# A planner that knows two more things about the chip: a port that VectorE and GpSimd share, and another pace of TensorE

## The chip, the core and the metric

The kernel runs on one core of a Trainium2 chip. A core has five engines with queues of their own: TensorE (PE: matmuls and transposes), VectorE (DVE), ScalarE (ACT), GpSimd (POOL) and SyncE (SP), which here issues most transfers. Each engine takes its instructions strictly in the order in which the program lists them, and an instruction whose operand isn't there yet holds up all behind it on that engine. The metric is the time of one execution in microseconds; the median of several runs counts.

## What is computed

One layer of a diffusion backbone over 1024 latent tokens of width 1024 and 256 context tokens, in float32:

```python
h, hc = modulate(rmsnorm(x)), modulate(rmsnorm(ctx))     # shifts, scales: silu(c) @ w_ada
q, k, v, z, xbc, dt, gates = split(h @ w_in)
o = diff_attention(rope(q), rope(k), v)                  # 8 heads, keys of context and latents
u = silu(dwconv3(xbc)); xs, B, C = split(u)              # SSD: 16 heads in 4 groups, chunks
y = scan_forward(xs, B, C, dt) + scan_backward(...) + d_skip * xs
y = group_rmsnorm(y * silu(z))
mix = (sig(ga) * (o @ w_attn) + sig(gs) * (y @ w_ssd)) @ w_out
x = x + gt1 * rmsnorm(mix)
f = shared_expert(h2) + top8_of_64_experts(h2)           # h2 = modulate(rmsnorm(x))
out = x + gt2 * rmsnorm(f)
```

## The kernel before

The program is one long stream in stages, which the profile shows one after the other: the modulation vectors and q, k, v (to about 400 us); the SSD **mixer** (400 to 1055); the branch projections and the attention (1055 to 1680); merge, output projection and routing (to about 1890); the mixture of experts (to 2745); the last norm and the output.

Products that need full float32 are made of three matmuls in F32R (a float32 operand is split into a high and a low part, `hi` and `lo`; `acc` gets `hh*hi`, `hl*hi` and `hh*lo`, 128x512 each). The split is an ACT copy for `hi` and a DVE or POOL subtraction for `lo`.

**What sets the order.** No order is written out by hand. Each piece of work is a generator (a *stream*) that yields what it needs next: tiles, free buffers of a ring, an engine. `Flow` keeps a model of time beside the program: `Flow.op` charges each operation to its engine's clock (`s.clk`) and notes when its result is ready. `Flow.run` resumes the stream that can go on first by that model (of those that can go on at once, the one with the lowest priority number), and whatever the stream issues is appended to the queues of its engines, under a manual schedule. So the numbers in `mm` (L137), `_dve`, `tt`, `ptt` and their like are never executed: they decide which instruction stands ahead of which. Two helpers also choose an engine by the clocks: `copy` (DVE or ACT) and `either`/`sub` (DVE or POOL).

**The mixer.** `server` (priority 3, so whenever nothing more urgent can go on) works off 41 jobs: columns of `w_in` for the convolution (`conv`), for `z` and for the gates (`g`). Its matmuls write `acc`: 3632 in F32R, besides those of `dt`. Once a group of heads has its convolved channels, `group` transposes them, and for each of four pairs (two heads by two halves of the sequence) spawns two `unit`s and one `products`. A unit works through

```python
F.stt(W[:, c], s.ge, dt[...], W[:, c], ...)     # x4, after 4 F.ts
F.ptt(G, Rv[0], ac[...], ALU.subtract)          # POOL, R loaded from acd
F.stt(G[:, c], Rv[1][:, c], ac[...], G[:, c], ...) # x4
F.ptt(W, W, CB[...], ALU.mult)                  # POOL
F.act(G, G, AF.Exp); F.tt(W, W, G, ALU.mult)
```

and its `decays` make `R` by an ACT exponential and a POOL product. `products` then issues a group of 24 float32 matmuls of 128 columns into `py` (48 records in the trace), which read both units' `W` and `R`; there are 16 such groups. Rings limit how far units run ahead: `G` and `W` have two buffers, `R` six. After a group, `evac` makes `yt`; after four, `norm` sums squares (`aux<-cst,G`), takes a reciprocal root on DVE (`rs_y`), spreads it with PE transposes (`aux<-cst,rs_y`) and stores `yn`. When all four head groups are through, `branches` opens: it loads `yn` and weights, splits them (`bxh`, `bxl`, `bwh`, `bwl`) and issues the `bacc` matmuls; `attention_ahead` loads `qk` through POOL's queue for the scores (`sps`).

Elsewhere `wacc` are DVE sums over rows of `w_ada` that PE adds up into `adab`, among the q, k, v matmuls; `tr<-cst,r` are transposes of rotated q and k; in the mixture of experts PE waits at times for a split of gathered tokens (`xl`) or of hidden values (`hl`).

Of the kernel before, what the change touches and what calls it, by code (L numbers as in the profile page):

```python
# [16 lines left out]
PSUM = bass.MemoryType.PSUM  # L17
# [56 lines left out]
def _n(ap):  # L74
    return ap.tensor.name


class Ring:


    def __init__(s, F, pool, shape, dt, name, n):
        s.F, s.pool, s.shape, s.dt, s.name, s.n = F, pool, shape, dt, name, n
        s.free, s.at = n, [0.0] * n
# [22 lines left out]
class Flow:  # L106
# [7 lines left out]
    def __init__(s, nc):  # L114
        s.nc = nc
        s.clk = {"PE": 0.0, "DVE": 0.0, "ACT": 0.0, "POOL": 0.0, "DMA": 0.0}
        s.ready, s.last, s.hold, s.streams, s.seq = {}, {}, {}, [], 0
        s.later, s.pend, s.now, s.fresh = [], {}, 0.0, {}

    def op(s, eng, dur, out, ins):  # L120
        if out is not None and _n(out) in s.pend:
            s.flush(src=_n(out))
        t = s.clk[eng]
        more = 55.0 if eng == "PE" else 0.0
        for a in ins:
            t = max(t, s.ready.get(_n(a), 0.0) + more)
        if out is not None:
            t = max(t, s.fresh.pop(_n(out), 0.0))
        e = t + dur
        s.clk[eng] = e  # L130
        for a in ins:
            s.last[_n(a)] = max(s.last.get(_n(a), 0.0), e)
        if out is not None:
            s.ready[_n(out)] = max(e + s.LAT[eng], s.ready.get(_n(out), 0.0) if eng == "DMA" else 0.0)
            s.last[_n(out)] = max(s.last.get(_n(out), 0.0), e)

    def mm(s, out, l, r, start, stop, d=None):  # L137
        n = r.free_size()
        if d is not None:
            pass  # L140
        elif l.dtype == F32:
            d = max(4 * n / 2.4, 213.0)
        elif l.dtype == F32R:
            d = n / 2.4 + 2 if n >= 256 else 107.0 if n >= 192 else 213.0
        else:
            d = max(n / 2.4, 27.0)
        s.nc.tensor.matmul(out, l, r, start=start, stop=stop)  # L147
        s.op("PE", d, out, (l, r))
# [14 lines left out]
        s.nc.scalar.copy(out, in_)  # L163
        s.op("ACT", (51 if in_.space == PSUM else 94) + 0.833 * out.free_size(), out, (in_,))

    def _dve(s, out, ins, rate=0.96, aps=0, base=65):
        s.op("DVE", base + 62 * aps + out.free_size() / rate, out, ins)

    def tt(s, out, a, b, op):
        s.nc.vector.tensor_tensor(out, a, b, op=op)  # L170
        s._dve(out, (a, b), base=69)

    def ptt(s, out, a, b, op):
        s.nc.gpsimd.tensor_tensor(out, a, b, op=op)
        s.op("POOL", 36 + 2.22 * out.free_size(), out, (a, b))

    def ts(s, out, a, s1, s2, op0, op1=None):
        if op1 is None:
            s.nc.vector.tensor_scalar(out, a, s1, s2, op0=op0)  # L179
        else:  # L180
            s.nc.vector.tensor_scalar(out, a, s1, s2, op0=op0, op1=op1)  # L181
        aps = [v for v in (s1, s2) if hasattr(v, "tensor")]
        s._dve(out, (a, *aps), 0.96 if a.space == PSUM else 1.92, len(aps))

    def stt(s, out, a, sc, b, op0, op1):
        s.nc.vector.scalar_tensor_tensor(out, a, sc, b, op0=op0, op1=op1)  # L186
        aps = (sc,) if hasattr(sc, "tensor") else ()
        s._dve(out, (a, b, *aps), aps=len(aps), base=69)

    def ts_reduce(s, out, a, s1, op0, op1, acc):  # L190

# [3 lines left out]

    def vcopy(s, out, a):
        s.nc.vector.tensor_copy(out, a)  # L197
        s._dve(out, (a,), 0.96 if a.space == PSUM else 1.92)

    def red(s, out, a, op):  # L200
        s.nc.vector.tensor_reduce(out, a, axis=AX.X, op=op)  # L201
# [2262 lines left out]
```

## Time and profile before

| what | value |
|---|---|
| three runs | 2828.54, 2836.93, 2843.67 us, median 2836.93 |
| the profiled execution | 2838.21 us, span of its trace 2836.1 us |
| mean granted clock of PE | 0.967 of full speed |
| PE busy | 2624.0 us, 93% of the span |
| DVE, ACT, POOL busy | 2000.2, 1339.9 and 882.9 us |
| DMA, 2250 to 2745 us | 96% of its engines' time, 304 GB/s |

The execution takes 2.1 us more than the span from its first to its last instruction. PE is busy nearly all the time, so the kernel's length is PE's work, plus the times that PE stands, plus what its matmuls lose at a lower clock. DVE, ACT and POOL stand often; that costs nothing unless PE waits for what they were late with.

### The profile page before, as it was taken

What the parts mean: (1) busy time and instruction counts of PE and PEld (TensorE: products, weight loads), DVE (VectorE), ACT (ScalarE), POOL (GpSimd) and SP (SyncE); (2) the same over time, 40 slices, a digit from 0 to 9 for tenths busy, and PEclk for the clock granted to TensorE, in tenths of its full rate; (3) what the DMA queues carried; (4) which work ended last, traced back from release to release, by engine and by line L of the source; (5) the groups of instructions that cost most, each with busy time, mean ns of one, the idle gap of its engine ahead of it and who ended that gap; (6) DMA issues with size and microseconds to landing.
All of it is one profiled execution on the core that took longest, in us unless ns stands there. A gap on an engine that the chain in (4) does not pass through costs nothing. (4 is left out here: it accounts for less than half of the span.)

```text
span 2836.1 us, 41280 instructions
## 1 busy us (share of the span) xinstructions
PE 2624.0 (93%) x14561; PEld 2109.4 (74%) x14561; DVE 2000.2 (71%) x4690; ACT 1339.9 (47%) x2105; POOL 882.9 (31%) x670
## 2 busy tenths in 40 slices
PE   7999979999999999999998899899999998999991
PEld 4777868878787776888887687678887776777660
DVE  6876123577776658888893657867788877787863
ACT  4211113344444445666673422335666656576641
POOL 0101010444454520000000000056656656666641
PEclk9999989999999999999999999999999999999995
DMA  7667242243424345224234853478899998999997
GB/s 278 211 205 201 84 127 84 75 130 93 134 82 138 101 133 183 88 84 145 92 101 152 266 164 109 184 247 250 278 310 302 316 302 266 308 305 312 327 306 212
DMA packets 275266, 544.89 MB, mean 192 GB/s; under 512 B 31546, under 2 KB 166819, under 8 KB 248050
## 3 DMA queue, kind: packets, MB, share of 16 engines
q1 hardware_dynamic: 238898, 435.31, 45.1%
q0 software_dynamic: 36160, 106.93, 14.8%
q8 instruction: 115, 1.88, 0.3%
q14 instruction: 93, 0.76, 0.1%
HBM read 432.99 MB, written 124.73 MB: 197 GB/s over the span
## 5 line engine op out<-in xcount | busy, mean ns | idle before, releaser
L170 DVE TENSOR_TENSOR gl<-raw,gh 128x1024 fp32r<-128x1024 f32 x240 | 288.3, 1218 | 40.4 <-ACT gh L163 40.2
L147 PE MATMUL acc<-hh,hi 128*128 128x512 f32 (+2 forms) x760 | 303.7, 400 | 1.4 <-DVE ux L186 1.4
L163 ACT CAST gh<-raw 128x1024 fp32r<-128x1024 f32 x240 | 247.6, 1051 | 101.2 <-PE gu L147 65.9
L147 PE MATMUL acc<-hl,hi 128*128 128x512 f32 (+2 forms) x760 | 287.8, 379 | 0.0
L147 PE MATMUL gu<-gh,xh 128*128 128x512 f32 (+3 forms) x672 | 280.7, 418 | 3.8 <-ACT xh L163 3.4
L147 PE MATMUL acc<-hh,lo 128*128 128x512 f32 (+1 forms) x736 | 279.3, 380 | 2.5 <-DVE lo L170 2.5
L147 PE MATMUL gu<-gl,xh 128*128 128x512 f32 (+3 forms) x672 | 266.7, 397 | 4.4 <-DVE gl L170 4.3
L147 PE MATMUL gu<-gh,xl 128*128 128x512 f32 (+3 forms) x672 | 266.9, 397 | 3.8 <-DVE xl L170 3.7
L261 POOL DMA_INDIRECT cr<-cumd,crow x98 | 124.8, 1273 | 440.7 <-DVE y L197 408.8
L192 DVE TENSOR_SCALAR_CACHE_REDUCE e<-sps 128x512 f32<-128x512 f32 (+1 forms) x384 | 214.2, 596 | 31.2 <-PE sps L147 31.0
L267 POOL DMA_INDIRECT yacc<-y,tk x98 | 180.4, 1841 | 86.3 <-issue 31.3
L147 PE MATMUL sps<-qk 128*128 128x512 f32 (+1 forms) x768 | 195.4, 385 | 8.2 <-DVE e L192 4.5
L155 ACT ACTIVATE e<-e,st 128x1280 f32<-128x1280 f32 x128 | 174.7, 1366 | 31.2 <-DVE st L201 31.0
L147 PE MATMUL acc<-hi,hh 128*128 128x512 f32 x448 | 183.3, 409 | 0.0
L261 POOL DMA_INDIRECT wc<-wtab,tk x98 | 137.9, 1407 | 141.3 <-DVE tk L181 93.9
L147 PE MATMUL acc<-hi,hl 128*128 128x512 f32 x448 | 177.3, 396 | 0.4 <-DVE hl L170 0.4
L147 PE MATMUL acc<-lo,hh 128*128 128x512 f32 x448 | 177.1, 395 | 0.0
L147 PEld LDWEIGHTS sps<-qk 128*128 128x128 f32 x768 | 140.0, 190 | 41.7 <-DVE e L192 10.8
L147 PEld LDWEIGHTS acc<-hh,hi 128*128 128x128 f32 (+1 forms) x760 | 143.5, 189 | 31.2 <-issue 3.7
L147 PE MATMUL pv<-wr,vv 128*128 128x256 f32 x640 | 164.2, 380 | 0.0
L147 PEld LDWEIGHTS acc<-hl,hi 128*128 128x128 f32 (+1 forms) x760 | 143.7, 189 | 25.3 <-issue 0.6
L147 PEld LDWEIGHTS acc<-hh,lo 128*128 128x128 f32 x736 | 139.6, 190 | 29.7 <-DVE lo L170 3.0
(323 smaller groups left out, 6253.7 us busy)
## 6 DMA issues: line engine op xcount, KB each, us to landing
raw<-in_w_e_gate_dram SPq DMA_DIRECT2D x64, 1024.0 KB, 10.6
raw<-in_w_e_up_dram SPq DMA_DIRECT2D x64, 1024.0 KB, 11.3
draw<-in_w_e_down_dram SPq DMA_DIRECT2D x64, 1024.0 KB, 10.0
qk<-qk POOLq DMA_DIRECT2D x16, 1664.0 KB, 8.4
raw<-in_w_in_dram SPq DMA_DIRECT2D x40, 512.0 KB, 4.6
wada<-in_w_ada_dram SPq DMA_DIRECT2D x32, 512.0 KB, 5.2
R<-acd SPq DMA_DIRECT2D x64, 256.0 KB, 5.4
qk<-sa SPq DMA_DIRECT2D x52, 256.0 KB, 4.3
```

Of the source, the lines that this page charges most:

```text
L147: s.nc.tensor.matmul(out, l, r, start=start, stop=stop)
L155: s.nc.scalar.activation(out, in_, fn, **kw)
L163: s.nc.scalar.copy(out, in_)
L170: s.nc.vector.tensor_tensor(out, a, b, op=op)
L192: s.nc.vector.tensor_scalar(out, a, s1, None, op0=op0, op1=op1, accum_out=acc)
L261: s.nc.gpsimd.indirect_dma_start(out=out, out_offset=None, in_=table, in_offset=bass.IndirectOffsetOnAxis(ap=idx, axis=0), **kw)
L267: s.nc.gpsimd.indirect_dma_start(out=table, out_offset=bass.IndirectOffsetOnAxis(ap=idx, axis=0), in_=in_, in_offset=None, compute_op=ALU. ...
```

## The change

`Flow` gets two more pieces of knowledge. `port` keeps the last eight intervals of each of DVE and POOL in which an operation holds the port that both use, and a new operation of the one starts, in the model, only after those of the other that it would overlap. Marked are POOL's `ptt` and, on DVE, `tt`, `stt`, `ts` and `vcopy` where no operand is in PSUM; not marked are reductions, reciprocals and indirect transfers. And an F32R matmul of n columns is charged (n+32)/2.4 ns in place of n/2.4+2: 226.7 in place of 215.3 for 512 columns. Nothing that is computed changes.

```diff
--- before.py
+++ after.py
@@ -115,9 +115,10 @@
         s.nc = nc
         s.clk = {"PE": 0.0, "DVE": 0.0, "ACT": 0.0, "POOL": 0.0, "DMA": 0.0}
         s.ready, s.last, s.hold, s.streams, s.seq = {}, {}, {}, [], 0
-        s.later, s.pend, s.now, s.fresh = [], {}, 0.0, {}
-
-    def op(s, eng, dur, out, ins):
+        s.later, s.pend, s.now, s.fresh, s.port = [], {}, 0.0, {}, {"DVE": [], "POOL": []}
+
+    def op(s, eng, dur, out, ins, port=False):
+
         if out is not None and _n(out) in s.pend:
             s.flush(src=_n(out))
         t = s.clk[eng]
@@ -126,6 +127,11 @@
             t = max(t, s.ready.get(_n(a), 0.0) + more)
         if out is not None:
             t = max(t, s.fresh.pop(_n(out), 0.0))
+        if port:
+            for a, b in sorted(s.port["POOL" if eng == "DVE" else "DVE"]):
+                if a < t + dur and t < b:
+                    t = b
+            s.port[eng] = s.port[eng][-7:] + [(t, t + dur)]
         e = t + dur
         s.clk[eng] = e
         for a in ins:
@@ -141,7 +147,7 @@
         elif l.dtype == F32:
             d = max(4 * n / 2.4, 213.0)
         elif l.dtype == F32R:
-            d = n / 2.4 + 2 if n >= 256 else 107.0 if n >= 192 else 213.0
+            d = (n + 32) / 2.4 if n >= 256 else 107.0 if n >= 192 else 213.0
         else:
             d = max(n / 2.4, 27.0)
         s.nc.tensor.matmul(out, l, r, start=start, stop=stop)
@@ -163,16 +169,16 @@
         s.nc.scalar.copy(out, in_)
         s.op("ACT", (51 if in_.space == PSUM else 94) + 0.833 * out.free_size(), out, (in_,))
 
-    def _dve(s, out, ins, rate=0.96, aps=0, base=65):
-        s.op("DVE", base + 62 * aps + out.free_size() / rate, out, ins)
+    def _dve(s, out, ins, rate=0.96, aps=0, base=65, port=False):
+        s.op("DVE", base + 62 * aps + out.free_size() / rate, out, ins, port)
 
     def tt(s, out, a, b, op):
         s.nc.vector.tensor_tensor(out, a, b, op=op)
-        s._dve(out, (a, b), base=69)
+        s._dve(out, (a, b), base=69, port=PSUM not in (a.space, b.space))
 
     def ptt(s, out, a, b, op):
         s.nc.gpsimd.tensor_tensor(out, a, b, op=op)
-        s.op("POOL", 36 + 2.22 * out.free_size(), out, (a, b))
+        s.op("POOL", 36 + 2.22 * out.free_size(), out, (a, b), True)
 
     def ts(s, out, a, s1, s2, op0, op1=None):
         if op1 is None:
@@ -180,12 +186,12 @@
         else:
             s.nc.vector.tensor_scalar(out, a, s1, s2, op0=op0, op1=op1)
         aps = [v for v in (s1, s2) if hasattr(v, "tensor")]
-        s._dve(out, (a, *aps), 0.96 if a.space == PSUM else 1.92, len(aps))
+        s._dve(out, (a, *aps), 0.96 if a.space == PSUM else 1.92, len(aps), port=a.space != PSUM)
 
     def stt(s, out, a, sc, b, op0, op1):
         s.nc.vector.scalar_tensor_tensor(out, a, sc, b, op0=op0, op1=op1)
         aps = (sc,) if hasattr(sc, "tensor") else ()
-        s._dve(out, (a, b, *aps), aps=len(aps), base=69)
+        s._dve(out, (a, b, *aps), aps=len(aps), base=69, port=PSUM not in (a.space, b.space))
 
     def ts_reduce(s, out, a, s1, op0, op1, acc):
 
@@ -195,7 +201,7 @@
 
     def vcopy(s, out, a):
         s.nc.vector.tensor_copy(out, a)
-        s._dve(out, (a,), 0.96 if a.space == PSUM else 1.92)
+        s._dve(out, (a,), 0.96 if a.space == PSUM else 1.92, port=a.space != PSUM)
 
     def red(s, out, a, op):
         s.nc.vector.tensor_reduce(out, a, axis=AX.X, op=op)
```

Instruction counts hardly change: PE's stay as they are, one `bwl` goes from DVE to POOL, three `Bn` copies from DVE to ACT and one `xn` copy the other way, and ACT loads its tables 71 times in place of 60. What changes is the order. Three places:

**PE among the q, k, v matmuls**, around the 12th `wacc` sum, which follows 372 F32R matmuls before (`acc` matmuls of one token tile, then the sum, then the next tile's):

```order
L147 MATMUL acc<-hi_732,hl_84 128x512
L147 MATMUL acc<-hi_732,hh_83 128x512
L147 MATMUL acc<-lo_733,hh_83 128x512
L147 MATMUL acc<-hi_732,hl_84 128x512
L147 MATMUL adab<-cst,wacc 128x1
L147 MATMUL acc<-hi_839,hh_83 128x512
L147 MATMUL acc<-lo_840,hh_83 128x512
L147 MATMUL acc<-hi_839,hl_84 128x512
```

and now, where it follows 384:

```order
L153 MATMUL acc<-lo_825,hh_83 128x512
L153 MATMUL acc<-hi_824,hl_84 128x512
L153 MATMUL acc<-hi_824,hh_83 128x512
L153 MATMUL acc<-lo_825,hh_83 128x512
L153 MATMUL acc<-hi_824,hl_84 128x512
L153 MATMUL acc<-hi_824,hh_83 128x512
L153 MATMUL acc<-lo_825,hh_83 128x512
L153 MATMUL acc<-hi_824,hl_84 128x512
L153 MATMUL adab<-cst,wacc 128x1
L153 MATMUL acc<-hi_732,hh_85 128x512
L153 MATMUL acc<-lo_733,hh_85 128x512
L153 MATMUL acc<-hi_732,hl_86 128x512
```

It stands 12 matmuls later. The fifth does too (240, now 252), and the 26th stands 36 later (612, now 648).

**PE at the mixer's end.** Before, the last product group follows 3449 conv and gate matmuls (`acc`), and 183 of them are left to stand behind it, around the norm's sums and transposes and around the first three branch matmuls; this is the piece with those:

```order
L147 MATMUL acc<-hh_85,hi 128x512
L147 MATMUL acc<-hl_86,hi 128x512
L147 MATMUL acc<-hh_85,lo 128x512
L147 MATMUL bacc<-bxh,bwh 128x512
L147 MATMUL bacc<-bxl,bwh 128x512
L147 MATMUL bacc<-bxh,bwl 128x512
L147 MATMUL acc<-hh_83,hi 128x512
L147 MATMUL acc<-hl_84,hi 128x512
L147 MATMUL acc<-hh_83,lo 128x512
```

Now all 3632 `acc` matmuls stand ahead of the third and the fourth group of the last four, which follow each other; after their 48 matmuls (the second group's last ones are shown) come the sums, the transposes and the branch matmuls with nothing between:

```order
L153 MATMUL py<-W,xn 64x128 x2
L153 MATMUL py<-R,hp_7664 64x128 x2
L153 MATMUL py<-R,hp_7665 64x128 x2
L153 MATMUL py<-W,xn 64x128 x2
L153 MATMUL py<-R,hp_7664 64x128 x2
L153 MATMUL py<-R,hp_7665 64x128 x2
L153 MATMUL aux<-cst,G 128x1 x8
L157 MATMUL aux<-cst,rs_y 128x128 x8
L153 MATMUL bacc<-bxh,bwh 128x512
L153 MATMUL bacc<-bxl,bwh 128x512
L153 MATMUL bacc<-bxh,bwl 128x512
```

Counted by the `acc` matmuls ahead of them, the four last groups stood at 3281, 3338, 3392 and 3449; now at 3497, 3578, 3632 and 3632. The twelve earlier ones are 48 to 191 later too (the first at 1985, was 1937), and the spacing inside a head group is 54 to 96, was 54 to 72.

**SP at the mixer's end.** Before, loads of weights (`raw`) and stores of gates (`gt`) stand around the stores of the normed result (`yn`):

```order
L211 DMA raw<-in_w_in_dram 128x8x128
L211 DMA gt_3154<-zg 128x512 x2
L211 DMA gt_3155<-zg 128x512
L211 DMA yn_3132<-yt 128x512
L211 DMA yn_3133<-yt 128x512
L211 DMA yn_3132<-yt 128x512
L211 DMA yn_3133<-yt 128x512
L211 DMA gt_3155<-zg 128x512
L211 DMA lv_8486<-in_lam_q_dram 128x64
L211 DMA lv_8487<-in_lam_k_dram 128x64
L211 DMA lv_8488<-in_lam_q_dram 128x64
L211 DMA lv_8489<-in_lam_k_dram 128x64
```

Now the last two loads of `R` (for the last unit) come right ahead of the stores of `yn`, and the gates are stored before:

```order
L217 DMA gt_3157<-zg 128x512
L217 DMA zg<-zs_3141 128x512
L217 DMA R<-acd_3124 128x512
L217 DMA R<-acd_3125 128x512
L217 DMA yn_3132<-yt 128x512
L217 DMA yn_3133<-yt 128x512
L217 DMA yn_3132<-yt 128x512
L217 DMA yn_3133<-yt 128x512
L217 DMA lv_8618<-in_lam_q_dram 128x64
L217 DMA lv_8619<-in_lam_k_dram 128x64
L217 DMA lv_8620<-in_lam_q_dram 128x64
L217 DMA lv_8621<-in_lam_k_dram 128x64
```

In the attention, the output projection and the mixture of experts the matmuls keep nearly the same distances from what they read: some sums of `xl` stand further ahead of their readers, some of `hl` a little nearer.

## Rows read from the trace of the kernel before

**Rows 1.** Page: span, and each engine's busy time.

```profile
span 2836.1 us, 41280 instructions
...
PE 2624.0 (93%) x14561; PEld 2109.4 (74%) x14561; DVE 2000.2 (71%) x4690; ACT 1339.9 (47%) x2105; POOL 882.9 (31%) x670
```

**Rows 2.** Windows: length, then PE, PEld, DVE, ACT, POOL busy, PEclk, DMA.

```profile
500.00:1055.00 555.00, 527.71 (x3039) 440.46 (x3037) 385.94 (x929) 243.83 (x350) 242.93 (x206) 0.98 0.35 108
...
2250.00:2745.00 495.00, 467.19 (x3134) 340.52 (x3134) 395.21 (x696) 312.20 (x486) 308.14 (x210) 0.98 0.96 304
```

**Rows 3.** Waits of PE, 500 to 1070: total us, times, longest.

```profile
PE py L147 <- DVE W L170: 14.0, 9, 2.9
PE py L147 <- POOL R L174: 8.0, 10, 3.3
PE acc L147 <- DVE lo L170: 2.5, 1, 2.5
```

**Rows 4.** Timeline of PE: start, duration, what ran.

```profile
1009.64 0.39 PE L147 MATMUL acc<-hh,lo 128*128 128x512 f32 x1
...
1011.45 0.39 PE L147 MATMUL acc<-hl,hi 128*128 128x512 f32 x1
...
1014.74 0.63 PE L147 MATMUL acc<-hh,hi 128*128 128x512 f32 x1
1015.17 0.63 PE L147 MATMUL acc<-hl,hi 128*128 128x512 f32 x1
```

**Rows 5.** Tile G, 500 to 1055: min/median/max duration in ns.

```profile
L186 DVE SCALAR_TENSOR_TENSOR G<-R,ac,G x128: 332/342/1382, 548.0 to 1012.4; 128x128 f32<-128x128 f32 x128
```

**Rows 6.** Timeline of PE, last product group.

```profile
1017.44 0.69 PE L147 MATMUL py<-W,xn 128*64 128x128 f32 x4
...
1020.49 0.50 PE L147 MATMUL acc<-hh,hi 128*128 128x512 f32 x1
```

**Rows 7.** Tile py on PE, 956.2 to 959.5.

```profile
L147 PE MATMUL py<-W,xn x13: 272/273/323, 956.4 to 959.5; 128*64 128x128 f32 x13
```

**Rows 8.** Tile py on PE, 973 to 982.

```profile
L147 PE MATMUL py<-W,xn x16: 272/417/473, 973.6 to 981.4; 128*64 128x128 f32 x16
```

**Rows 9.** Timeline of PE, first branch matmul.

```profile
1055.30 0.51 PE L147 MATMUL bacc<-bxh,bwh 128*128 128x512 f32 x1 [1.12 <-ACT bxh L163]
```

**Rows 10.** Timeline of DVE, mixer's end; wait in brackets.

```profile
1022.78 1.29 DVE L170 TENSOR_TENSOR lo<-raw,hi 128x512 fp32r<-128x512 f32 x2 [5.57 <-ACT hi L163]
1023.99 0.74 DVE L186 SCALAR_TENSOR_TENSOR yt<-yt,dcol,py 128x512 f32<-128x512 f32 x1
...
1034.74 1.29 DVE L170 TENSOR_TENSOR lo<-raw,hi 128x512 fp32r<-128x512 f32 x2
...
1039.44 1.41 DVE L186 SCALAR_TENSOR_TENSOR yt<-yt,vcol,aux 128x512 f32<-128x512 f32 x2 [2.53 <-PE aux L151]
```

**Rows 11.** Timeline of POOL, before the load of qk.

```profile
1060.68 1.29 POOL L174 TENSOR_TENSOR bxl<-braw,bxh 128x512 fp32r<-128x512 f32 x1 [29.50 <-ACT bxh L163]
```

**Rows 12.** Page, DMA issues: us to landing.

```profile
qk<-qk POOLq DMA_DIRECT2D x16, 1664.0 KB, 8.4
```

**Rows 13.** Timeline of PE, first score matmul.

```profile
1075.06 1.76 PE L147 MATMUL sps<-qk 128*128 128x512 f32 x8
```

**Rows 14.** Timeline of ACT, a table load.

```profile
1049.44 1.28 ACT L155 ACT_TABLE_LOAD   x1
```

**Rows 15.** Waits of PE, 100 to 410.

```profile
PE adab L147 <- DVE wacc L186: 7.9, 3, 4.7
PE tr L151 <- POOL r L174: 4.6, 3, 2.5
```

**Rows 16.** Timeline of DVE, before the 12th sum's wait.

```profile
146.64 0.29 DVE L179 TENSOR_SCALAR wacc<-wada,cc 128x128 f32<-128x128 f32 x1 [6.70 <-DMA wada<-in_w_ada_dram]
```

**Rows 17.** Waits of PE, 1680 to the end.

```profile
PE xt L151 <- DVE xl L170: 10.8, 5, 5.4
PE dn L147 <- DVE hl L170: 9.1, 6, 2.8
```

## Prediction

> **What bounds the kernel now.** I read the page first: PE is busy for 2624.0 of 2836.1 us, no other engine for more than 71% [rows 1]. So the time is PE's work plus PE's standing, and a change of order can move only the second, 212 us, and what matmuls lose at a lower clock. The windows say where [rows 2]: in the mixer, 500 to 1055 us, PE is busy for 527.71 of 555 us, so it stands 27.3 us; from 2250 to 2745 us it stands 27.8 us, but there the DMA engines are busy 96% of the time, and an order brings little. The waits of PE in the mixer name the reason [rows 3]: 14.0 us for `W` from DVE, 8.0 us for `R` from POOL, 2.5 us for `lo`, together 24.5. They are many and short, 20 of them, none over 3.3 us. The reader is to see that `py` is late by little each time: PE comes to a product group before its unit is through.
>
> The timeline shows what a wait costs beside itself [rows 4]. In an undisturbed stretch eight steps of 512-column matmuls take 1011.45 - 1009.64 = 1.81 us, 226 ns each. After the wait for `lo` one step takes 1015.17 - 1014.74 = 0.43 us: PE runs at the lower of its two levels (1.2 GHz), and seven matmuls are paid nearly double, 1.4 us in all.
>
> **The change part by part.**
>
> *PE's pace.* The old price is 215.3 ns, the new one 226.7, the trace's 226 [rows 4]. So the old model's PE gets through 512 columns 11.4 ns too early, 41 us over the mixer's 3632 conv and gate matmuls, and to fill the time of a unit on DVE and POOL it puts 5% more matmuls ahead of its products than fit, some 3 of 60, 0.7 us. That was a cushion for a late unit. The new price alone would take it away: this part speaks for longer waits, not shorter ones. The Trainium skill, "TensorE: Matmul & The Clock Gate", section Back-to-back issue gap, gives N/2.4 + 2.5 ns for a lone warm matmul, 215.8 ns at 512 columns, by which the old price is the right one and the new one 5% too dear; by it the 183 matmuls below would take an estimated 39.5 us, and the forecast would come out 2 us lower. The trace of this case does not agree: 226 against 215.8, and the measurement decides.
>
> *The shared port.* DVE's `stt` into `G` takes 332 ns at least, 342 in the median and 1382 at most [rows 5]: the slow ones stand some 1040 ns for another's use. No term of the old model has that. The new one gives both engines later ends, so units come out later in the model, and by more than the new pace takes back: more conv matmuls are put ahead of each product group (spacing 54 to 96, was 54 to 72), and the conv matmuls run out earlier: none is left behind the last two groups, where 183 were.
>
> *The mixer's sum.* The standing that goes is at most 24.5 us [rows 3]. For the slow steps the granted clock bounds the price: 0.98 over 555 us [rows 2] means about 4% of it at half speed, 22 us, of which half, 11, is lost. I take 35 for both; if a third of it stays, all times below are 12 us later, and that is the third rival. The last group starts at 1017.44, and PE goes on at 1020.49, so a group costs 3.0 us [rows 6]. PE reaches the new third group at 1017.4 - 35 - 3.0 + 183 x 0.226 (41.4) = 1020.8, and the second, which has 54 matmuls (12.2) and a group less ahead of it, at 1005.6.
>
> The fourth can't follow at once. `G` and `W` have two buffers, which the two units of one pair fill, so pair after pair must pass the chain on DVE, POOL and ACT. Its pace: groups of the last four start at 956.4 and 973.6, 17.2 apart [rows 7, 8], and then at 1017.44, two further on, 21.9 each [rows 6]. POOL's own work is 242.93 us over 16 pairs, 15.2 each [rows 2]. I take 17.2, since the conv's splits no longer lie between, with 15.2 and 21.9 as ends: the fourth group starts at 1005.6 + 34.4 = 1040.0 (1036.0 to 1049.4). So the chain, which conv matmuls covered, ends 23 us later than before, with PE standing.
>
> Then the tail. Before, from the last group's start to the first branch matmul it is 1055.30 - 1017.44 = 37.9 us [rows 6, 9], under cover of the 183 matmuls. Part of it is the cover's own doing [rows 10]: DVE's sum of `yt` comes at 1023.99, 3.5 us after the group's end, behind splits for the conv; another split, 1.3 us, lies in the reciprocal root; and `yt` waits 2.5 us for transposes that stand behind `acc` in PE's queue. These 7.3 us go; 30.6 are left. The score matmuls wait for more: casts of `yn` until POOL's `bxl` at 1060.68 (5.4 us behind the first branch matmul), that itself, 1.3 us [rows 11], and the load of `qk` that is issued behind it in POOL's queue, 8.4 us [rows 12]. Together 45.7 (39.0 if neither `bxl` nor the casts hold up the load, 53.0 if none of the 7.3 goes). The first score matmul comes at 1085.7, 1075.06 before [rows 13]: **+10.6 us** (1036.0 + 39.0 = 1075, 0; 1049.4 + 53.0 = 1102.4, +27).
>
> Eleven more table loads on ACT, 1.28 us each [rows 14], cost nothing in the mixer, where ACT works 243.83 of 555 us [rows 2]; without that cover, in the tail, one or two could stand, up to 2.6 us, inside the upper end. On SP the last loads of `R` come right ahead of `yn`, with no `raw` load or gate store between any more; the loads for the branches stand behind `yn` as before.
>
> *The q, k, v stage.* PE waits 7.9 us in three waits for `wacc`, the longest 4.7, and 4.6 in three for `r` [rows 15]. The three sums stand 12, 12 and 36 matmuls later: 2.7, 2.7 and 8.1 us at 226 ns. That takes all but 2 us of the longest: 7.9 - 2.0 = 5.9. The two longer waits each have slow steps behind them, 1.4 us by the count above; I credit one, and nearly 1 us for `r`. **-8 us** (-11 if all goes with both clocks). What speaks against it: DVE stood 6.70 us for `wada`, a transfer, ahead of the sum that PE waited for longest [rows 16]; if transfers set that pace, the wait comes back at the new place, and -2 is left.
>
> *Attention, and from the output projection on.* The attention's order keeps its distances: 0. Behind it PE waits 10.8 us for `xl` and 9.1 for `hl` [rows 17]. The sums of `xl` stand further ahead at the worst places, those of `hl` a little nearer; a third of the first goes: **-3 us** (-10 if nearly all goes, +8 if `hl` nearly doubles). The transfers at 96% take part of any gain there.
>
> Sum: -8 + 10.6 - 3 = -0.4, on the profiled 2838.2 us: 2837.8. The median of the runs is 1.3 us below the profiled one, so 2836.5, told as 2836.
>
> **The rivals.**
>
> *Faster: the tail is cheap.* With no conv to split, DVE, ACT and POOL have nothing but the last two pairs; at POOL's own 15.2 us a pair and the short tail of 39.0 the first score matmul comes at 1075, no later than before, and the gains of the other stages count: -11 to -8, and -3 to -10, so 2817 to 2826, about 2820. For it speaks that POOL works only 44% of the mixer's time. Against it that a pair is a chain over three engines and a transfer, and that no gap between the last groups was under 17.2.
>
> *Slower: the mixer's end lies open.* Place: behind the last `acc` matmul. Price: pairs at 21.9 and a tail of 53.0 give +27, and PE, which has stood, starts the branches at the lower level. With -2 in the q, k, v stage and nothing later it is 2838.2 - 1.3 + 25 = 2862; with -8 and -3, 2853. It decides when the first score matmul comes later than about 1100 us on the clock of before (1075 + 14 + 11 of gains).
>
> *The change removes waits only in part.* The port as the chip grants it follows no order that the planner knows, and a DVE operation that takes 342 or 1382 ns [rows 5] can be late at the new place too. With a third of the 35 us left, 12 us, and all else as forecast it is 2848. For it speaks that a group's two units are never apart by the same time; against it that most groups now stand 6 us of matmuls further back (the spacing of up to 96 against 72, 24 matmuls, 5.4 us), more than the longest wait of 3.3.
>
> **How the numbers follow.** Three runs of before spread over 15 us, so a change under 0.5%, 14 us, can hardly be told from none. Forecast 0.46, faster rival 0.29, slower rival 0.17, waits left in part 0.08. Within 0.5% of 2836.9 is 2822.7 to 2851.1. Of the faster rival's 2817 to 2826 a third lies within, so 0.19 is left; the slower rival counts in full. Of the forecast a tenth is credited to faster, its small terms all going one way, 0.05, and 0.02 to slower. That makes faster 0.24, same 0.57, slower 0.19. The range leaves out a tenth at either side: from 2815, below the faster rival's 2817, to 2859, between the slower rival's two values. The likeliest case's own range is 2824 to 2848.
>
> **What would show it.** Right: PE's waits for `W` and `R` between 500 us and the third of the last four groups fall from 22 to under 8 us; one long wait stands ahead of the fourth group, 12 to 25 us, and one or two ahead of the first branch and score matmuls, with the granted clock low in that stretch; `wacc` waits under 3 us. The first score matmul comes some 3 us later than before on the new clock (10.6 - 8). Wrong would be: many short waits for `W` as before, with matmuls of the conv run out all the same (then it is slower); a fourth group less than 12 us behind the third (faster); waits for `hl` over 15 us.

## The result and the profile after

The changed kernel takes 2910.49 us in the median of four runs (2906.49 to 2916.91), the kernel before 2833.86 in its four; the ratio is 1.026 (1.0237 to 1.0283). It is slower by some 77 us, outside the range that I gave. The page of after, beside [rows 1]:

```profile
span 2915.1 us, 41287 instructions
...
PE 2639.9 (91%) x14561; PEld 2118.3 (73%) x14561; DVE 1997.2 (69%) x4687; ACT 1354.8 (46%) x2118; POOL 893.8 (31%) x671
```

PE does 16 us more by its records (its mean granted clock is 0.955, was 0.967), but the span grew by 79. Where, the first matmuls of each stage tell. This table is counted from the traces: a stage ends where the next one's first matmul starts (first `acc<-hh,hi`, `sps`, `gu<-woh`, `xt<-cst,xg`; the experts end with the last `gu<-raw`). The rows below those two are the runs of the experiments.

```
                q,k,v   mixer  attention  out   experts   end    span
before          400.7   674.4    593.9   112.9    990.7   63.6   2836.1
after           391.6   704.9    609.1   113.6   1030.9   65.0   2915.1
e1_pace         403.0   709.0    596.8   113.6   1031.7   63.9   2918.1
e2_port         388.4   713.3    601.8   112.9    982.7   64.0   2863.1
e3_pace204      395.2   704.7    612.0   112.2    986.9   64.3   2875.2
e4_pace238      409.7   717.4    602.3   114.3   1047.3   64.6   2955.6
e5_pace216      399.9   673.7    592.3   112.9   1000.0   67.9   2846.8
e6_slack        391.4   702.7    605.2   113.6   1055.0   65.1   2933.0
e7_softport     391.9   685.1    607.3   112.9    993.2   64.2   2854.6
e8_port_qkv     388.1   673.9    596.0   112.9    998.1   64.0   2832.9
e9_after_ind    392.6   704.4    603.4   113.6   1090.4   67.7   2972.1
e10_qkv_ind     385.9   674.1    594.9   112.9   1087.8   68.9   2924.5
e11_early       385.8   719.0    598.8   112.9    981.0   64.2   2861.8
e12_before_dup  417.9   676.8    594.9   112.9    998.2   63.7   2864.5
e13_after_dup   408.4   703.8    605.1   113.9   1041.6   64.0   2936.9
e14_before_copy 402.3   672.5    595.0   112.9   1027.8   63.7   2874.1
e15_after_copy  391.3   706.4    603.4   113.6   1066.9   64.8   2946.5
e16_pace209     395.7   709.0    598.9   112.3    991.6   64.2   2871.7
e17_pace221     402.1   709.7    597.4   113.4   1017.9   63.9   2904.3
e18_pace232     407.9   703.7    597.7   113.4   1006.5   64.2   2893.4
```

From before to after: -9 in q, k, v, +30 in the mixer, +15 in the attention, +1 in the output, +40 among the experts and +1 at the end; that is the 79. Kernels whose experts stand in the order of before (e2, e7, e8, e11) take 981 to 998 us there, so a difference of some 15 us between two traces in that column says nothing. The mixer and the attention repeat better: four more kernels with after's order up to the experts (e6, e9, e13, e15) take 703 to 706 and 603 to 605 us, four with before's order there (e8, e10, e12, e14) 673 to 677 and 595 to 596. So the mixer's 30 us are sure, and of the attention's 15 some 7 to 10.

The windows of after, in the columns of [rows 2]: the mixer's main part, its end, and the experts from first to last:

```profile
500.00:1055.00 555.00, 520.33 (x2974) 434.35 (x2973) 371.09 (x898) 255.94 (x356) 228.61 (x204) 0.97 0.35 105
1060.00:1100.00 40.00, 17.66 (x64) 12.31 (x63) 14.83 (x37) 7.64 (x13) 5.30 (x6) 0.70 0.59 199
1819.20:2850.20 1031.00, 953.42 (x5749) 729.28 (x5748) 773.96 (x1473) 577.75 (x899) 586.23 (x390) 0.97 0.85 275
```

and the last two of before, at about the same distance from the first score matmul and over the same stage:

```profile
1038.00:1078.00 40.00, 38.60 (x174) 31.08 (x172) 14.31 (x31) 14.99 (x23) 4.03 (x5) 1.00 0.77 265
1781.90:2772.60 990.70, 942.30 (x5748) 723.95 (x5748) 775.07 (x1474) 577.95 (x899) 563.86 (x390) 0.98 0.89 287
```

In the mixer's main part PE is busy for 520 of 555 us, was 528; then come 40 us with 17.7 busy, at a granted clock of 0.70, where before was busy for 38.6 at the full clock. Among the experts PE stands 77.6 us, was 48.4: that is 29 of the 40, and the other 11 are its matmuls, which take longer at the lower clock. DMA's share fell from 0.89 to 0.85 there. The waits of PE from 396 us to the third of the last four product groups at 1031.1, which answer to [rows 3]:

```profile
PE aux L153 <- ACT G L169: 12.9, 1, 12.9
PE py L153 <- POOL R L180: 8.3, 6, 3.2
PE acc L153 <- DVE lo L176: 5.2, 3, 2.2
PE acc L153 <- DVE ux L192: 4.6, 2, 2.3
```

The reader is to see what is missing and what isn't: no wait for `W` is left (14.0 before), but those for `R` are as before (8.3 and 8.0), and the conv's own matmuls now wait for DVE, `lo` and `ux` together 9.8 us where it was 3.9: the 2.5 of [rows 3] and

```profile
PE acc L147 <- DVE ux L186: 1.4, 1, 1.4
```

Then the timeline of PE at the mixer's end, beside [rows 6, 9, 13]:

```profile
1031.12 0.84 PE L153 MATMUL py<-W,xn 128*64 128x128 f32 x3
...
1036.48 0.48 PE L153 MATMUL py<-R,hp 128*64 128x128 f32 x1 [3.28 <-POOL R L180]
...
1048.41 0.66 PE L153 MATMUL py<-W,xn 128*64 128x128 f32 x2 [7.39 <-DVE W L176]
1053.91 0.47 PE L153 MATMUL py<-W,xn 128*64 128x128 f32 x1 [4.84 <-DVE W L176]
...
1082.41 0.79 PE L153 MATMUL bacc<-bxh,bwh 128*128 128x512 f32 x1 [12.85 <-ACT bxh L169]
...
1096.49 0.74 PE L153 MATMUL sps<-qk 128*128 128x512 f32 x2 [1.21 <-DMA qk<-qk]
```

The fourth group stands 7.39 and 4.84 us for `W`, the first branch matmul 12.85 us for a cast of `yn`. And the waits of PE from the routing's end on, beside [rows 17]:

```profile
PE hT L157 <- DVE hid L176: 29.6, 13, 4.7
PE dn L153 <- ACT hh L169: 8.2, 4, 6.8
PE xt L157 <- DVE xl L176: 8.2, 3, 4.7
PE hT L157 <- DVE tk L187: 6.0, 2, 3.5
...
PE dn L153 <- DVE hl L176: 3.1, 3, 1.3
```

`xl` and `hl` fell from 10.8 and 9.1 to 8.2 and 3.1. The new one is `hid`, the hidden values before their transposes: 29.6 us in 13 waits. Before it was

```profile
PE hT L151 <- DVE hid L170: 5.5, 4, 3.9
```

### The profile page after: what moved, and what is told of

Read it like the earlier page. It is cut to its first block, busy times and chain, and to the rows that moved or that the text cites. A ratio compares the mean times of both kernels' runs of the same rounds, so it can differ in the third digit from the quotient of the medians.

```text
span 2915.1 us, 41287 instructions
## 1 busy us (share of the span) xinstructions
PE 2639.9 (91%) x14561; PEld 2118.3 (73%) x14561; DVE 1997.2 (69%) x4687; ACT 1354.8 (46%) x2118; POOL 893.8 (31%) x671
## 4 chain that ended last, share of the span: by engine, by line
PE 52%; DMA 15%; DVE 8%; issue 5%; POOL 3%; ACT 2%; SPq 1%; POOLq 0%; ACTq 0%; DVEq 0%
PE acc L153 12%; PE gu L153 11%; PE dn L153 6%; PE bacc L153 5%; DMA yacc<-y,tk 5%; PE sps L153 5%; PE pv L153 4%; DMA cr<-cumd,crow 4%; PE tr L157 2%; PE aux L153 2%; PE xt L157 2%; PE py L153 1%; DVE gl L176 1%; SPq L217 1%; DVE W L185 1%
## 5 line engine op out<-in xcount | busy, mean ns | idle before, releaser
L273 POOL DMA_INDIRECT yacc<-y,tk x98 | 194.8, 1988 | 96.7 <-ACT y L161 41.0
L153 PE MATMUL sps<-qk 128*128 128x512 f32 (+1 forms) x768 | 195.4, 388 | 10.8 <-DVE e L198 6.8
L267 POOL DMA_INDIRECT wc<-wtab,tk x98 | 144.8, 1477 | 167.8 <-DVE tk L187 107.2
L153 PEld LDWEIGHTS sps<-qk 128*128 128x128 f32 x768 | 142.3, 193 | 41.4 <-DVE e L198 10.1
```

What stands on the lines that cost most here:

```text
L267: s.nc.gpsimd.indirect_dma_start(out=out, out_offset=None, in_=table, in_offset=bass.IndirectOffsetOnAxis(ap=idx, axis=0), **kw)
L273: s.nc.gpsimd.indirect_dma_start(out=table, out_offset=bass.IndirectOffsetOnAxis(ap=idx, axis=0), in_=in_, in_offset=None, compute_op=ALU. ...
```

## The experiments

Two parts were changed at once, so each was run alone first. Their orders tell something before any time does: in e1 the matmuls stand as in the changed kernel from the output projection to the end, one by one, and in e2 as in the kernel before. From the experts on the traces show the same of DVE, ACT, POOL and SP.

**e1_pace** and **e2_port**, one part each:

```diff
-        if port:                                  # e1, against after
+        if False:
-            d = (n + 32) / 2.4 if n >= 256 else ...  # e2, against after
+            d = n / 2.4 + 2 if n >= 256 else ...
```

> New price of TensorE alone, no port in the model; the order of the matmuls from the output projection on is then the same as in the changed kernel, and the attention's nearly so. Theory A (the old, too low price was a cushion for late operands; the true price takes it away): attention 14 to 16 us and experts 40 to 44 us longer than before, as in the changed kernel, mixer within 10 us of before, total 2875 to 2900. Theory B (the port's part does it, through the clocks of VectorE and GpSimd): attention and experts as before within 8 us, total 2825 to 2845.

> The port alone, old price of TensorE; the order from the output projection on is that of the kernel before. Theory A: attention and experts as before within 8 us; the mixer 20 to 40 us longer, since the last three product groups stand behind all conv matmuls; total 2850 to 2875. Theory B: total 2885 or more.

Measured: 2915.77 us, 1.0279 (1.0255 to 1.0302), and 2871.43 us, 1.0134 (1.0108 to 1.0159). The table splits the loss. The experts' 40 us come with the price of PE alone (1031.7 in e1, 982.7 in e2): that is shown, since every queue stands there as in after or as in before; the waits for `hid` go with it, 26.8 us in e1 and 4.0 in e2. The gain in q, k, v comes with the port alone (388.4; with the price alone it is 403.0). The mixer loses with either, 35 and 39 us, and no more with both: e1 misses there what theory A expected (within 10 us), and with it in the total. The attention's 15 us are not the price's either, against A: with nearly the same order it takes 596.8 us in e1 and 609.1 in after. What differs is how it starts: in after PE waits at once for weights that are loaded behind the mixer's late end,

```profile
1106.12 0.80 PE L153 MATMUL bacc<-bxh,bwh 128*128 128x512 f32 x1 [8.17 <-ACT bwh L169]
```

and that is more than half of the 15 us; the rest is spread. The order of before fares alike: behind a mixer that ends open, with 12.8 and 13.0 us of waits for `bxh`, it takes 601.8 us in e2 and 607.3 in e7, and 593.9 in before.

**e3_pace204**, **e4_pace238**, **e5_pace216**, and later **e16_pace209**, **e17_pace221** and **e18_pace232**: the kernel before with another price alone.

```diff
-            d = n / 2.4 + 2 if n >= 256 else ...
+            d = n / 2.4 - 9.4 if n >= 256 else ...   # e4 + 24.8, e5 + 3, e16 - 4.0, e17 + 7.7, e18 + 19.1
```

> The kernel before with a still lower price of TensorE, 203.9 ns for 512 columns. If the low price is a cushion (A), the experts take no longer than the 1054 us of before by more than 8 us and the attention neither; total 2815 to 2845. If any change of the numbers shuffles the order of the experts with an outcome that has no direction (C), the experts' time lies 15 us or more away on either side, as likely as not.

> The kernel before with a price above the measured one, 238.1 ns. A: the experts take at least as long as in the changed kernel, 1090 us or more, and the attention 610 or more; total 2880 to 2940. C: no direction; the experts' time is as likely below 1085 as above.

> The kernel before with a price of 216.3 ns in place of 215.3; the mixer's matmul order stays nearly the same, that of the experts is reshuffled about as much as by the whole change. Theory A (a price below the chip's pace is a cushion; one ns is nothing): experts, from their first transposes on, 1054 us as before within 10 us, total within 12 us of before. Theory C (any reshuffling costs, since the other constants were found for just this order): experts 20 us or more longer, total 2855 or more.

> The kernel before with a price of 209.3 ns. Experts: 987 us at 203.9, 991 at 215.3, 1000 at 216.3, 1031 at 226.7 and 1047 at 238.1 so far. If the price has a direction (A in its weak form): 980 to 1002. If reshuffling alone decides (C): outside that. Mixer: 685 or more, as in every order but one so far.

> Price 221.0 ns. Direction: experts 1003 to 1030 us. C: outside that. Mixer 685 or more.

> Price 232.4 ns. Direction: experts 1031 to 1050 us. C: outside that. Mixer 685 or more.

(The 1054 and 1096 us in these texts count the experts to the end of the span.) Measured: 2885.13, 2953.09 and 2856.68 us (ratios 1.0175, 1.0415 and 1.0044), and one run each of the last three, 2873.5, 2906.07 and 2895.13 (before beside them, also one run: 2841.58). In order of the price, 203.9 to 238.1 ns, the experts take 987, 992, 981 to 998 (before's price), 1000, 1018, 1031, 1006 and 1047 us. No price below 217 gave more than 1000 us, none above it less than 1006, so there is a direction; but 232.4 breaks the row, so the single value is not to be trusted by 20 us. The one nanosecond of e5 reshuffles the experts as much as the whole change does. It costs them some 9 us by the traces, no more than that column spreads, and 0.44% in all: more than A expected, less than C. So reshuffling as such (C) is not the 40. Of the expectations e16 and e17 came out as the direction had it and e18 against it; the totals of e3 and e4 lie above A's, by 40 and 13 us, since the mixer lost 30 and 43 us in them; and the attention doesn't follow the price, 612.0 us at the lowest and 602.3 at the highest.

The mixer is another matter. Of these six, only e5, which keeps before's order there but for 80 of 3542 places, keeps its 674 us; the others take 704 to 717, at lower prices and at higher ones.

**e6_slack**: the cushion given back by hand, among the experts alone.

```diff
-SLACK = 400.0, 0.0, 200.0, ...
+SLACK = 1200.0, 500.0, 600.0, ...
```

> The changed kernel with larger constants by which the model holds the experts' products back behind their operands: 1200, 500 and 600 ns in place of 400, 0 and 200 (hidden values, their low part, tokens). Only the order from the experts on differs. A: the cushion comes back; PE's waits for hidden values fall from 30 to under 12 us, the experts take 1050 to 1075 us in place of 1096, total 2870 to 2890. Rival D (the transfers under load set the experts' pace, so PE waits whatever stands ahead): waits move to other operands, experts 1085 us or more.

Measured: 2932.81 us, 1.0307 (1.0272 to 1.0341); experts 1055 us to the last `gu`, 24 more than after (1120 to the end of the span, as the expectation counts). The waits of PE there:

```profile
PE hT L157 <- DVE hid L176: 19.0, 12, 3.8
PE dn L153 <- DVE wc L292: 12.2, 2, 7.7
PE dn L153 <- ACT y L161: 10.1, 3, 5.9
```

`hid` fell by a third and others came in its place. So the theory that I had most trust in, that PE's matmuls only stand too near to their operands, falls: more distance made it longer. Rival D came out as it said, waits for other operands and more than 1085 us; its cause, the transfers' load, is what e14 and e15 ask about. I looked at one of the waits for `hid` in the timeline of after, first on PE:

```profile
2506.81 0.40 PE L153 MATMUL gu<-gh,xl 128*128 128x512 f32 x1
2511.89 0.64 PE L157 MATMUL hT<-cst,hid 112*128 112x112 f32 x2 [4.68 <-DVE hid L176]
```

then on DVE:

```profile
2508.95 2.36 DVE L176 TENSOR_TENSOR gl<-raw,gh 128x1024 fp32r<-128x1024 f32 x2 [4.60 <-ACT gh L169]
2511.22 0.61 DVE L176 TENSOR_TENSOR hid<-gu,sg 112x256 f32<-112x256 f32 x1
```

and on ACT:

```profile
2507.29 0.69 ACT L161 ACTIVATE y<-dn,wc 128x512 f32<-128x512 f32 x1 [8.24 <-PE gu L153]
2507.88 2.92 ACT L169 CAST gh<-raw 128x1024 fp32r<-128x1024 f32 x3
2510.71 0.38 ACT L161 ACTIVATE sg<-gu 112x256 f32<-112x256 f32 x1
```

`hid` stands on DVE behind `gl` splits, those wait for ACT's `gh` casts, and `sg`, which `hid` needs, stands on ACT behind three of them; ACT in turn stood 8.24 us in front of `y`. The bracket names PE, since PE's count was the last to rise, at 2507.23; but the last matmul of `dn` had ended at 2498.89. What `y` had waited for besides, by the trace, was the indirect store that last read its buffer: issued at 2495.86, its sixteenth and last part landed at 2507.19. So in this wait the operand's own engines were held up at the head of their queues, by a transfer. Over the stage ACT's waits for an indirect store to free `y`, and DVE's for an indirect load of `cr`, are

```profile
ACT y L161 <- DMA yacc<-y,tk: 70.6, 18, 7.7
```

and

```profile
DVE cr L185 <- DMA cr<-cumd,crow: 58.6, 27, 5.7
```

together 129 us, and 72 in the kernel before:

```profile
ACT y L155 <- DMA yacc<-y,tk: 34.9, 14, 7.7
DVE cr L179 <- DMA cr<-cumd,crow: 37.3, 18, 6.8
```

**e9_after_ind** and **e10_qkv_ind** tried whether these are the cause (theory D here, another than the rival D of e6), with a planner that knows how long such transfers take; e10 is e8 (below) with the same two lines:

```diff
         s._dma(out, table, at=s.clk["POOL"] - 450.0)
+        s.ready[_n(out)] += 6000.0        # gather
         s._dma(table, in_, at=s.clk["POOL"] - 450.0)
+        s.last[_n(in_)] += 8000.0         # scatter_add
```

> The changed kernel, in whose model an indirect load is ready 6 us later and the source of an indirect store is free 8 us later (the traces show 8 to 11 us from issue to landing, the model has about 3). Only the order from the experts on differs from the changed kernel. Theory D (ACT's and DVE's queues are held up by instructions that wait for indirect transfers, put there too early): ACT's waits for y and DVE's for cr fall from 131 us to under 90, the experts take 1000 us or less in place of 1031, total 2870 to 2885. Theory A (only the distance of PE's matmuls from their operands counts): 1025 us or more, 2900 to 2920.

> The kernel with the port for the q, k, v stage alone, with the same two latencies of indirect transfers; up to the experts it is the order of that kernel. D: the waits for y and cr fall from 64 us to under 50, the experts take 970 to 990 us in place of 998, total 2805 to 2822. A: no gain, or a reshuffling that costs: 2825 to 2850.

Measured: 2971.55 us, 1.0486 (1.0453 to 1.0518), and 2932.83 us, 1.0355 (1.0328 to 1.0382). The waits went, as D wanted:

```profile
ACT y L161 <- DMA yacc<-y,tk: 14.0, 3, 6.8
```

and

```profile
DVE cr L185 <- DMA cr<-cumd,crow: 14.7, 4, 6.0
```

28.7 us in e9 in place of 129. And the experts took 1090 and 1088 us, 60 and 90 more than in after and in e8; both totals lie far above what either theory gave. PE now waits elsewhere, in e9:

```profile
PE gu L153 <- ACT gh L169: 33.3, 10, 9.4
PE dn L153 <- ACT y L161: 31.8, 13, 7.4
PE hT L157 <- DVE hl L176: 14.4, 8, 3.7
```

So D falls too as the cause: those waits go with slow orders, but an order without them is slower still. These edits too changed the whole order, so they don't tell what the waits cost in an order that is kept.

**e12_before_dup**, **e13_after_dup**, **e14_before_copy**, **e15_after_copy** asked whether transfers bound the stage (T): both kernels with 25 MB of copies that nothing reads, so nothing of the output changes.

```diff
+    nc.sync.dma_start(s.dram(f"dup_{n}_{r}", [P, 256]), ...[:, :256])              # e12, e13: each load
+    if "gate" in n: nc.scalar.dma_start(s.dram(f"dup_{r}", [P, 768]), ...[:, :768]) # e14, e15: each expert
```

> The kernel before with one more transfer behind each load of expert weights, a copy of an eighth of the matrix to a place in DRAM that nothing reads: 25 MB more. The order of the matmuls is unchanged. Theory T (the experts are bound by transfers, which starve where buffers come free late): DMA is full already, so the experts take 60 to 90 us longer. Theory O (the waits lie in the engines' queues): less than 40 us longer.

> The changed kernel with the same 25 MB more. T: its DMA engines stand 9 to 13% of the late stretch, which takes up part of the copies: 25 to 55 us longer, so that the 40 us between the two kernels' experts shrink to 20 or less. O: it grows by as much as the kernel before, and the 40 us stay within 10.

> The kernel before with one copy of 384 KB to a place in DRAM per routed expert, 25 MB in all, issued from ACT's queue, where it stands behind the expert's loads in the program's order, so that it runs in the experts' stage; matmul order unchanged. Theory T (transfers bound the stage): experts 60 to 90 us longer. Theory O (queues bound it): less than 40 us longer.

> The changed kernel with the same copies. T: transfers have room, so 25 to 55 us longer, and the 40 us between the two kernels' experts shrink to 20 or less. O: longer by as much as the kernel before, the 40 us stay within 10.

e12 and e13 say nothing: SyncE's queue has no manual order, and the copies ran in the q, k, v stage, which grew by 17 us in both (2870.05 and 2945.73 us). In e14 and e15 (2876.25, 1.0097, and 2957.35, 1.0376) they ran among the experts: that stage went from 990.7 to 1027.8 and from 1030.9 to 1066.9 us, 37 and 36. The distance of the two kernels stays at 39, though after had more room in its DMA. That speaks for O, the order in the queues. With two reserves: issuing a copy holds ACT for 0.5 us, 32 us for the 64, which may be the whole growth; and beside these two the kernel before took 2849.63 us, more than in the result, so that e14 is only 27 us longer than it.

**e7_softport** and **e11_early** are about the mixer, with the port alone at the old price:

```diff
-                if a < t + dur and t < b:
+                if a <= t < b:                                                # e7
-            yield [hp[0], hp[1], *(F.ready[_n(q)] + 400.0 for v in ready ...)]
+            yield [hp[0], hp[1], *(F.ready[_n(q)] - 4000.0 for v in ready ...)] # e11
```

> The port alone, old price, and an operation of the model is moved only behind one of the other engine that already runs when it starts, not behind one that would start while it runs. Only the mixer's order (and a little of the stage before) differs from before; conv matmuls per head group are 474, against 417 before and 504 with the port as changed. Theory L (products placed later free W and R later, so the units follow the matmuls' pace): 143 to 147 us from head group to head group, against 134 and 152; mixer 688 to 705 us. Rival P (VectorE and GpSimd pace the units by themselves): 134 us, mixer 680 or less.

> The port alone, old price, with the products let go 4 us before their operands are ready in the model, in place of 0.4 us behind. Only the mixer's order differs from the kernel with the port alone; conv matmuls per head group are 456, against 504 there. L (late products free their buffers late): 134 to 140 us from head group to head group, against 152, though PE waits 15 us or more longer for W and R; mixer 680 to 692 us against 713. Rival P (units are slow by themselves): PE's new waits come on top, 150 us or more, mixer 710 or more.

Measured: 2858.74 us, 1.0053 (1.0036 to 1.007), mixer 685.1; and 2861.61 us, 1.0096 (1.0063 to 1.0129), mixer 719.0. From the first product group of one head group to that of the next it takes 129 to 135 us before, 149 to 155 in e2, 138 to 143 in e7 and 139 to 145 in e11. e7 lies between the two theories, nearer to L, whose ranges (143 to 147, 688 to 705) it just misses; in e11 the period fell nearly as L had it, the mixer did not. The waits of PE in its mixer:

```profile
PE py L153 <- POOL R L180: 22.3, 10, 4.2
PE acc L153 <- DVE ux L192: 18.8, 5, 7.3
PE bacc L153 <- ACT bxh L169: 7.8, 1, 7.8
PE acc L153 <- DVE uB L192: 6.9, 3, 2.3
```

and in that of e1:

```profile
PE py L153 <- DVE W L176: 22.7, 9, 4.4
PE acc L153 <- DVE ux L192: 22.6, 5, 6.1
```

With early products the conv's matmuls wait for their banks, which DVE's `ux` sums free: 22.6 us in e1 and 18.8 in e11, and 1.4 before. That DVE does the units' work first there is how I read it. So there are two ways to lose some 30 us: products late, and the mixer's end lies open (after, e2); products early, and the conv waits for DVE (e1, e3, e4, e11, e16, e17, e18). L comes near for the period but does not explain the mixer's length.

**e8_port_qkv**: the port in the model only until the mixer begins, at the old price.

```diff
-        if port:
+        if port and s.locked:
             s.norm_and_qkv()
+            s.F.locked = False
```

> The port alone, and only up to the end of the q, k, v stage; from the mixer on the order is that of the kernel before, matmul for matmul. Theory A and L alike: the stage is 10 to 13 us shorter (12 with the port alone), nothing else moves: 2822 to 2828, ratio 0.995 to 0.997. Rival: the mixer starts earlier but its transfers don't, and the gain is lost at its start: 2834 to 2840.

Measured: 2826.06 us, 0.9934 (0.991 to 0.9957), against 2846.04 of the kernel before beside it: faster than both kernels, by little. The stage takes 388.1 us in place of 400.7, and all behind it stands in the old order. In the one trace, of a run of 2835.25 us, the experts took 998.1 us, at the upper end of what that order takes, and the span is only 3 us shorter than that of before; the gain of 12 to 26 us that the interval gives rests on the medians, and the stage explains 12.6 of it. The waits of PE there, 12.5 us before [rows 15], are

```profile
PE tr L157 <- POOL r L180: 2.5, 1, 2.5
PE adab L153 <- DVE wacc L192: 1.8, 1, 1.8
```

## Why the prediction was wrong

The trace's span came out 79 us longer than the forecast had it: -1 in q, k, v, 20 in the mixer, 15 in the attention and 45 behind it.

**q, k, v: right.** -8 was forecast, -9.1 came; the waits for `wacc` and `r` fell from 12.5 to 5.9 us.

```profile
PE adab L153 <- DVE wacc L192: 3.4, 5, 1.4
PE tr L157 <- POOL r L180: 2.5, 1, 2.5
```

The bound of -2, by which transfers would bring the waits back, did not come true.

**The mixer: wrong in its first step, right in the steps behind.** "The standing that goes is at most 24.5 us [rows 3] ... I take 35 for both" failed. Up to the third of the last groups PE's waits fell from 38.8 us (26.3 without the one for `G` at the start) to 31.3 (18.4): 7.5 us, since `R` stayed and `ux` and `lo` rose. PE reached that group 639.5 us after the mixer's first matmul; by before's 616.75 + 41.4 - 3.0 it would have been 655.1. So 15.6 us went, slow steps included, not 35. I took every wait of the row for one that ends when its reader is moved back, and did not ask what else the same change moves. (The readers did move: counted in the traces the twelve earlier groups stand 48 to 225 `acc` matmuls later, not 48 to 191 as I wrote above.) Why `R` stayed isn't shown. What I said of the price alone, longer waits, e1 bears out: 22.7 us for `W`, 14.0 before. The rest of the sum held: the fourth group came 17.3 us behind the third (17.2 taken per pair, though from the second on), and the first score matmul 48.1 us behind its start (45.7, bounds 39 to 53). On the clock of before it came at 1105.6, not 1085.7; the 19.9 us between are the first step's 19.4 and little else. My third rival had the mechanism, waits left in part, at a third of the 35; more than half were left. And by the test that I gave the slower rival, a first score matmul later than about 1100 us on the clock of before, that rival came true: 1105.6. Of the signs of being right that I named, the waits came near (`W` and `R` 8.3 us against under 8, `wacc` 3.4 against under 3), but the one wait ahead of the fourth group was 7.4 us, not 12 to 25, and on the new clock the first score matmul came 21 us later than before, not 3.

**The attention: its 0 was wrong by 15.** I compared the matmuls' distances and found them kept, and the new order as such costs little, 3 us in e1. But an order that is kept still starts from where the stage before leaves the engines: e1 shows nearly the same order 12 us shorter behind a mixer that ends covered, and e2 and e7 the order of before 8 and 13 us longer behind one that ends open. My slower rival named the open end; its price stopped at the first score matmul.

**From the output projection on: wrong by 45.** "A third of the first goes: -3 us (-10 if nearly all goes, +8 if `hl` nearly doubles)." What the step said of its rows came true for `xl`, which fell by 2.6 us; `hl` fell by 6.0, though its sums stand a little nearer. But the step listed only the two largest waits of PE as if they were the stock that the change could draw on; the 29.6 us for `hid` are new, and in the one that I followed the origin was two queues further back. That the new price as such costs this stage about 40 us is shown (e1 against e2, with the same orders as after and before on every engine). Why is not settled: not the amount of transfers as far as e14 and e15 tell, not only the distance of PE's matmuls (e6), not the waits for indirect transfers by themselves as far as e9 and e10 tell. What is left is argued: a planner that believes PE slower sees more idle time on ACT and DVE, and each setting that made the model later (a higher price, larger constants, honest latencies) gave the experts a slower order. Another reading is left untested: the model's other constants were fitted to the old order, so that most ways off it cost; against it speak e3 and e16, at lower prices, whose experts took 987 and 992 us.

**The rule of the Trainium skill** that I weighed, in "TensorE: Matmul & The Clock Gate", section Back-to-back issue gap, is for a lone matmul, 215.8 ns; taken for a stream it would have the old price right. The trace of after says 226 ns a step, as that of before did. But the question was the wrong one: the better price made the worse order in e1, and e17 and e18, 6 ns to either side of it, were slower than before too.

The slower rival came nearest, at 2853 to 2862 us; with the experts' 40 and the attention's 15 it comes to 2908 to 2917. Nothing in my range stood for a loss of more than 8 us from the output projection on. Without the experts' 40 the time would have been 2870 us, still 11 above my range; without the attention's 15 as well 2855, just inside.

## What to carry to other kernels

A planner whose other constants were found with a wrong price in place may not be improved by the right one, as here: correct one number, then time each stage, since every order behind it changes. The largest waits in a profile are no list of what a new order can cost; ask of each stage what stands ahead, on the same in-order queue, of the operations that feed PE. And a correction that helps in one stage can be kept for that stage alone, as e8 did, if the order behind it is shown to be the old one.

## What was not expected of the hardware

The port shows only where all of DVE's operands lie in SBUF. Counted in the trace of before, 500 to 1055 us: of 96 `stt` operations into `G` that began while POOL worked 43% took over 150 ns longer than the shortest; of 182 into `hp`, which read a bank of PSUM, none did, and their mean was 3 ns above it. So in these two kinds the change marks the right one. Yet over that stretch all of DVE's operations together take 90 us more than the shortest of their kinds before, and 87 in after's mixer (490 to 1060 us): knowing of the port, the planner hardly avoids it.
